# The gates of a gated DeltaNet layer: context and latents in the two halves of each 32-row group, 256 columns instead of 512

## The chip, the core and the metric

The program runs on one core of a Trainium2 chip. The metric is the device time of one launch in microseconds (us). The core's engines work side by side, each through its own list of instructions in a fixed order: TensorE (PE in the profile, its weight loads PEld), VectorE (DVE), ScalarE (ACT), GpSimd (POOL) and SyncE, whose queue (SP) issues nearly all DMAs. An instruction that waits for another engine holds up everything behind it on its own engine.

## The reference, cut to what matters

Two layers run on 256 context tokens and 256 latent tokens of width 1024. Layer 0 is a state-space layer with an MLP, layer 1 a bidirectional gated DeltaNet (the recurrence layer) with an MLP. The change lies in the gates of layer 1: for every token, two directions and 16 heads, a write strength `beta` and a decay `g`, and the running sum of `g` within chunks of 64 tokens.

```python
gl = rest[..., qk + vd:].astype(f32).reshape(b, l, 2, 2, GDN_VALUE_HEADS)
beta = jax.nn.sigmoid(gl[:, :, 0])
g = -jnp.exp(a_log) * jax.nn.softplus(gl[:, :, 1] + dt_bias)
...
g_b = jnp.cumsum(blocks(g), axis=-1)          # blocks of GDN_CHUNK = 64 tokens
decay = jnp.exp(jnp.where(incl, g_b[..., :, None] - g_b[..., None, :], -jnp.inf))
lower = jnp.where(strict, jnp.einsum('nbhcd,nbhsd->nbhcs', k_beta, k_b) * decay, 0.0)
t_mat = triangular_solve(lower + eye, eye)    # then u, w, k_end, and the scan over chunks
```

The gate values `gl` are 64 columns of one product `h @ w_in` (kind of gate x direction x head).

## The kernel before

Layer 1 is one call of `gdn_phase`. It makes tasks, Python generators that emit instructions: one projection per 128 columns of `w_in` (`gdn_proj`, 48 of them and one for the gates), the work on each projection's result (`post_qk`, `post_z`, `post_v`, each with a five-tap convolution in `conv_silu`), the gates (`gdn_gates`), the triangular inverse per pair of heads and direction (`gdn_t`, 16 of them), the chunk recurrence per head (`gdn_chain`), the read-out and the output projection.

`drive` chooses the order in which the tasks emit. It keeps a model of every engine's time (`Clock.issue`, lines 170 to 255: a cost for each instruction from its number of columns), and takes the task that the model says can start first, by priority among equals; a scheduler then fixes each engine's list from these priorities. The list is static. When the model's cost of some instructions changes, the order of all that is emitted later can change, on all engines.

The gates go as follows. `gdn_proj` (line 1609) makes 48 matmuls of 256 columns, first on the latents, then on the context, into the two halves of one bank `proj` [128, 512]: the 128 rows are 4 groups of 32 (beta of direction 0 and 1, decay of direction 0 and 1), the 512 columns are the tokens. Only 16 rows of each 32 are heads; the other 16 have zero weights. `gdn_gates` (line 1506) works on [128, 512] tiles named `gt`: sigmoid and softplus by an exponential and a polynomial of the logarithm (lines 1522 to 1549, on DVE but for the exponential), the running sum `GR` by two scans over 32 rows (line 1558) with a mask that POOL sets (lines 1555 and 1556), its copy to DRAM `grd` by four DMAs (line 1564), its transposes `gtp` on PE (line 1568), and the sums at each chunk's end, `glp`, by 16 small products (line 1575). From these come `gpn`, `gn`, `egs`, `neg`, `egl` and `vsc`, small tiles that scale the recurrence.

Who needs them: each `gdn_t` loads a tile `X` from `grd` by DMAs of SP, adds a mask on POOL, subtracts `gpn` on DVE, takes the exponential on ACT, and then makes five rounds of a DVE transpose `T`, a product `ap` on PE, a mask on DVE (`A`) and a product `up`. It also needs `kks`, made from `kk`, the products of the normalised keys. The keys are normalised in `post_qk`: convolution (`cacc`, four steps of DVE), `kc`, transposes `kp`, `kn` and its sums of squares `kss` on ACT, `krs` on POOL, `kn` scaled on ACT, transposes `kTp` on PE.

Three more helpers set the pace. `w_split` turns each loaded weight block `wraw` into `whi` (ACT) and `wlo` (in this layer four POOL instructions of 256 columns per block); a projection needs both. A projection's bank (`proj`, or `c2` for the first ten in turn with it) is free again when ACT has copied it to one of two convolution buffers (`pp`). The projections come in the order q0, q1, gates, z0, z1, k0, v0, v1, k1, v2, v3 and so on, k, v and q standing for keys, values and queries.

Of the kernel before, what the change touches and what calls it, by code (L numbers as in the profile page):

```python
# [8 lines left out]
F32 = mybir.dt.float32  # L9
# [4 lines left out]
OP = mybir.AluOpType  # L14
# [964 lines left out]
def host_weights(i):  # L979
    a = {n: np.asarray(v) for n, v in i.items()}  # L980
    out = {}
    w = a["s5_w_glu"][0].reshape(8, 128, 2, 4, 256)
    out["w_glu"] = w.transpose(3, 0, 1, 2, 4).reshape(4, 4, 2, 128, 512).transpose(0, 1, 3, 2, 4).reshape(4, 4, 128, 1024)
    out["w1"] = a["mlp_w1"].reshape(2, 4, 2, 128, 8, 512).transpose(0, 4, 1, 3, 2, 5).reshape(2, 8, 4, 128, 1024)
    out["w2"] = a["mlp_w2"].reshape(2, 8, 4, 128, 1024)
    wi = a["gdn_w_in"][0]
    out["w_in"] = wi[:, :6144].reshape(8, 128, 48, 128).transpose(2, 1, 0, 3).reshape(48, 128, 1024)
    wg = np.zeros((1024, 4, 32), np.float32)
    wg[:, :, :16] = wi[:, 6144:].reshape(1024, 4, 16)
    out["w_gate"] = wg.reshape(8, 128, 128).transpose(1, 0, 2).reshape(128, 1024)  # L990
    gb = np.zeros((2, 4, 32), np.float32)
    gb[0, 2:, :16] = a["gdn_dt_bias"][0]
    gb[1, 2:, :16] = a["gdn_a_log"][0]
    out["gcol"] = gb.reshape(2, 128).T
    out["conv"] = a["gdn_conv_w"][0].reshape(5, 32, 128).transpose(2, 1, 0)
    out["onorm"] = a["gdn_onorm_w"][0].reshape(128, 1)
    out["w_out"] = a["gdn_w_out"][0].reshape(16, 128, 1024)
    out["fnorm"] = np.broadcast_to(a["final_norm_w"][None], (128, 1024))
    return {n: np.ascontiguousarray(v, dtype=np.float32) for n, v in out.items()}
# [428 lines left out]
def host_consts2():  # L1428
    c = np.zeros((128, NCONST2), np.float32)
    p = np.arange(128) % 64  # L1430
    J, I = p[:, None], np.arange(64)[None, :]
    for d in range(2):
        c[:, M_INC + 64 * d:M_INC + 64 * d + 64] = np.where((I >= J, I <= J)[d], 0.0, NEG)

        a, b = (J, I) if d == 0 else (I, J)
        c[:, M_U + 64 * d:M_U + 64 * d + 64] = (I == J) | ((a % 2 == 0) & (b == a + 1))

        i, j = (J, I) if d == 0 else (I, J)
        for n, s in enumerate((2, 4, 8, 16, 32)):
# [6 lines left out]
    c[:, M_G] = np.where(r % 32 >= 16, 0.0, np.where(r < 64, -1.0, 1.0))  # L1446
    c[:, M_G + 1] = (r % 32 < 16) & (r >= 64)
    return c


def host_layout2(i):
    out = host_weights(i)
    out["consts2"] = np.ascontiguousarray(host_consts2(), dtype=np.float32)
    return out


class K3(K2):
# [48 lines left out]
    def gdn_gates(self, tmp, o):  # L1506
        nc, V, G = self.nc, self.nc.vector, self.nc.gpsimd
        P, c2 = self.g, self.c2
        gc = tmp.tile([128, 2], F32, name="gc")
        nc.sync.dma_start(gc, self.I["gcol"])  # L1510
        ps, slot = o.pop("ps"), o.pop("slot")
        room = iter(("ub0", "ub1", "ub0", "ub1", "ub0", "ub1", "N", "N"))

        def t():
            tag = next(room)
            return (self.gb.tile([128, 512], F32, name="gt", tag=tag) if tag == "N" else
                    self.gw.tile([128, 512], F32, name="gt", tag=tag, bufs=NRB))


        gs, gm = c2[:, M_G:M_G + 1], c2[:, M_G + 1:M_G + 2]  # L1520
        s, a, e = t(), t(), t()
        V.tensor_scalar(s, ps, gs, gc[:, 0:1], op0=OP.mult, op1=OP.add)
        slot.give()
        V.scalar_tensor_tensor(a, s, -1.0, s, op0=OP.mult, op1=OP.max)
        nc.scalar.activation(e, a, AF.Exp, scale=-1.0)
        yield

        z, z2 = t(), t()
        q, r = a, t()
        V.tensor_scalar(z, e, 2.0, None, op0=OP.add)  # L1530
        V.reciprocal(z, z)
# [18 lines left out]
        GR = z2  # L1550
        V.tensor_copy(GR[0:64], lg[0:64])
        m = z
        for d in range(2):
            r = slice(64 + 32 * d, 96 + 32 * d)
            G.memset(m[r], 1.0)
            G.memset(m[r, (0 if d == 0 else 63):512:64], 0.0)
            f = lambda x: x[r] if d == 0 else bass.AP(tensor=x.tensor, offset=x[r].offset + 511, ap=[list(x[r].ap[0]), [-1, 512]])
            V.tensor_tensor_scan(f(GR), f(m), f(lg), 0.0, op0=OP.mult, op1=OP.add)
        self.grd = self.dram.tile([2, 16, 512], F32, name="grd")
        for d in range(2):  # L1560
            for h2 in range(2):
                r = 64 + 32 * d + h2
                dst = bass.AP(tensor=self.grd.tensor, offset=self.grd.offset + 8192 * d + 64 * h2, ap=[[1024, 8], [128, 8], [1, 64]])
                nc.sync.dma_start(dst, GR[r:r + 16:2].rearrange("p (c i) -> p c i", i=64))
        yield
        tp = self.tr("gtp")
        for b in range(4):
            nc.tensor.transpose(tp[:, b * 128:b * 128 + 128], GR[:, b * 128:b * 128 + 128], self.ident)
        lp = self.tr("glp")
        for k in range(8):  # L1570
            for d in range(2):
                c = k if d == 0 else (3 - k if k < 4 else 11 - k)
                last = c * 64 + (63 if d == 0 else 0)
                o = k * 32 + d * 16
                nc.tensor.matmul(lp[:, o:o + 16], GR[64:128, last:last + 1].to_broadcast([64, 128]),
                                 self.ident[64:128, 64 + 32 * d:64 + 32 * d + 16], start=(k == 0 and d == 0), stop=(k == 7 and d == 1),
                                 skip_group_check=True)
        gt = t().rearrange("p (a b c d) -> p a b c d", a=4, b=2, c=2)
        V.tensor_copy(gt.rearrange("p a b c d -> p (a b c d)"), tp)
        gl = t()[:, 0:256].rearrange("p (a b c) -> p a b c", a=8, b=2)  # L1580
        V.tensor_copy(gl.rearrange("p a b c -> p (a b c)"), lp[:, 0:256])

        self.gp = P.tile([128, 4, 2, 16], F32, name="gpn")
        V.tensor_tensor(self.gp, gt[:, :, 1, :, 0:16], gt[:, :, 0, :, 0:16], op=OP.subtract)
        self.egl = P.tile([128, 8, 2, 16], F32, name="egl")
        nc.scalar.activation(self.egl, gl, AF.Exp)

        gn = tmp.tile([128, 4, 2, 16], F32, name="gn")
        V.tensor_copy(gn, gt[:, :, 1, :, 0:16])
        self.egs = P.tile([128, 4, 2, 16], F32, name="egs")  # L1590
        self.vsc = P.tile([128, 4, 2, 16], F32, name="vsc")
        pr = lambda x: x.rearrange("p (a b) h -> p a b h", a=2)
# [15 lines left out]

    def gdn_proj(self, streams, out):

        while not self.wq:
            yield HOLD
        wh, wl = self.wq.pop(0)
        n, self.nproj = self.nproj, self.nproj + 1
        out["slot"] = slot = self.pslots[n % len(self.pslots) if n < NEARLY else 0]
        yield from slot.take()
        ps = self.bank("proj", "pr", bufs=NPR) if slot is self.pslots[0] else self.cb[-self.pslots.index(slot)]
        for n, s in enumerate(streams):
            o = ps if s is None else ps[:, 256 * s:256 * s + 256] if len(streams) > 1 else ps[:, 0:256]
            for dt in range(8):  # L1620
                self.mm3(o, wh[:, dt], wl[:, dt], self.cols(self.hh, dt, s), self.cols(self.hl, dt, s), dt == 0, dt == 7)
# [424 lines left out]
    def gdn_phase(self, tmp, gb, hp, new):  # L2046
        full, lat = (None,), (1,)
        I, T = self.I, Task
        st, blocks, pj, tasks, o = [dict() for _ in range(8)], [], [], [], {}
# [47 lines left out]
        g, j = g  # L2097
# [47 lines left out]
        dst = [hp.tile([128, 4, 1024], F32R, name=n, tag=n) for n in ("hh", "hl")]  # L2145
# [119 lines left out]
```

## Time and profile before

| what | us |
|---|---|
| median of three runs | 1602.71 |
| lowest and highest of the three | 1600.59 and 1606.34 |
| the profiled execution, as timed | 1608.33 |
| its span in the trace | 1606.5 |
| PE busy in the span | 1461.4 (91%) |
| DVE busy | 1098.4 (68%) |
| ACT busy | 775.2 (48%) |
| POOL busy | 652.0 (41%) |

The profile is one execution. Its timed value, 1608.33 us, is 1.8 us above its span and 5.6 us above the median of the runs. All times of the trace are us from the start of the span. Layer 1 begins at about 738 us and its output projection ends at about 1375 us. A busy share over the whole span says little here, as the stages have different limits; the stretches of 20 us below are read instead.

### The profile page before, as it was taken

To read this page: it belongs to the slowest core of one execution; us is meant where nothing else is said; L and a number is where in the kernel's file an instruction comes from. 1 tells how busy PE (TensorE), PEld (TensorE's weight loads), DVE (VectorE), ACT (ScalarE), POOL (GpSimd) and SP (SyncE) were. 2 spreads that over 40 slices of the span, in tenths; PEclk is the share of its full clock that TensorE was granted. 3 is DMA by queue.
4 is the path that set the end of the run, shared out by engine and by line. 5 is a ranking of instruction groups with operands and counts; after the bars stand their busy time and mean duration, and the time that the engine had idled before them with its cause. 6 is when DMAs were issued, how large, how long until landed. Compare 5 with 4: busy or idle time off the path is not lost. (4 is left out here: it accounts for less than half of the span.)

```text
span 1606.5 us, 31329 instructions
## 1 busy us (share of the span) xinstructions
PE 1461.4 (91%) x12370; PEld 1115.2 (69%) x12370; DVE 1098.4 (68%) x2036; ACT 775.2 (48%) x1635; POOL 652.0 (41%) x590
## 2 busy tenths in 40 slices
PE   6895689989999999996978998989998999989998
PEld 2474457768777777786756775767776665789997
DVE  6999877754334333448998876686978775666766
ACT  3262675534222223315456655656665755564443
POOL 4962026623333332335777543443543400024432
PEclk8897789989999999998889999989998999999999
DMA  8758725454444454422222211111121112535552
GB/s 286 255 195 200 141 86 184 151 183 134 163 162 166 163 187 161 152 91 66 90 70 67 67 54 48 50 51 54 61 70 38 45 58 79 188 127 194 185 186 92
DMA packets 76771, 200.77 MB, mean 125 GB/s; under 512 B 8784, under 2 KB 29008, under 8 KB 76368
## 3 DMA queue, kind: packets, MB, share of 16 engines
q1 hardware_dynamic: 76112, 197.78, 38.3%
q8 instruction: 97, 1.59, 0.4%
q10 hardware_dynamic: 512, 0.98, 0.2%
q14 instruction: 50, 0.41, 0.1%
HBM read 192.71 MB, written 6.03 MB: 124 GB/s over the span
## 5 line engine op out<-in xcount | busy, mean ns | idle before, releaser
L273 ACT CAST whi<-wraw 128x1024 fp32r<-128x1024 f32 x221 | 225.6, 1045 | 255.7 <-PE w L273 139.0
L273 POOL TENSOR_TENSOR wlo<-wraw,whi 128x256 fp32r<-128x256 f32 (+1 forms) x221 | 206.8, 963 | 270.7 <-ACT whi L273 253.2
L273 DVE TENSOR_TENSOR wlo<-wraw,whi 128x1024 fp32r<-128x1024 f32 (+1 forms) x189 | 223.4, 1210 | 81.5 <-ACT whi L273 80.6
L273 PE MATMUL w<-hh,whi 128*128 128x256 f32 (+1 forms) x512 | 170.4, 335 | 0.0
L273 PE MATMUL w<-hl,whi 128*128 128x256 f32 (+1 forms) x512 | 169.3, 332 | 0.0
L273 PE MATMUL w<-hh,wlo 128*128 128x256 f32 (+1 forms) x512 | 168.9, 332 | 0.0
L273 POOL TENSOR_TENSOR sq<-rl 128x512 f32<-128x512 f32 (+1 forms) x64 | 62.7, 980 | 216.1 <-ACT rl L273 212.1
L273 PE MATMUL w<-whi,h1h 128*128 128x512 f32 x384 | 148.9, 395 | 0.0
L273 PE MATMUL w<-whi,h1l 128*128 128x512 f32 x384 | 148.5, 390 | 0.0
L273 PE MATMUL w<-wlo,h1h 128*128 128x512 f32 x384 | 148.4, 389 | 0.0
L273 PE MATMUL proj<-hh,whi 128*128 128x256 f32 (+1 forms) x360 | 132.4, 368 | 7.4 <-ACT pp L273 6.7
L273 DVE TENSOR_TENSOR ma<-w,g 128x512 f32<-128x512 f32 x96 | 65.3, 687 | 103.0 <-PE w L273 102.9
L273 PE MATMUL proj<-hh,wlo 128*128 128x256 f32 (+1 forms) x360 | 127.8, 355 | 1.2 <-POOL wlo L273 1.2
L273 PE MATMUL proj<-hl,whi 128*128 128x256 f32 (+1 forms) x360 | 127.3, 354 | 0.0
L273 POOL TENSOR_TENSOR xr<-xr,ma 128x512 f32<-128x512 f32 x56 | 82.2, 1471 | 95.1 <-DVE ma L273 95.1
L273 DVE SCALAR_TENSOR_TENSOR cacc<-pp,cw,cacc 128x520 f32<-128x520 f32 (+1 forms) x128 | 112.3, 879 | 9.6 <-ACT cacc L273 8.0
L273 ACT ACTIVATE v<-c,vsc 64x128 f32<-64x128 f32 x224 | 80.7, 362 | 62.8 <-PE c L273 57.7
L273 PEld LDWEIGHTS w<-hh,whi 128*128 128x128 f32 x512 | 98.0, 192 | 18.3 <-DVE wlo L273 4.2
L273 DVE TENSOR_TENSOR h1l<-sq,h1h 128x512 fp32r<-128x512 f32 (+1 forms) x64 | 36.3, 568 | 104.5 <-POOL sq L273 102.1
L273 PEld LDWEIGHTS w<-hl,whi 128*128 128x128 f32 x512 | 98.5, 192 | 10.5 <-issue 1.9
L273 PEld LDWEIGHTS w<-hh,wlo 128*128 128x128 f32 x512 | 98.3, 192 | 9.8 <-issue 0.8
L273 POOL TENSOR_TENSOR rstd<-ms,mhalf 128x1 f32<-128x1 f32 (+2 forms) x22 | 17.3, 788 | 179.1 <-DVE ms L273 163.4
(316 smaller groups left out, 3492.2 us busy)
## 6 DMA issues: line engine op xcount, KB each, us to landing
wraw<-in_w_dram SPq DMA_DIRECT2D x128, 512.0 KB, 4.5
adaw<-in_ada_w_dram SPq DMA_DIRECT2D x92, 512.0 KB, 4.8
wraw<-in_w_in_dram SPq DMA_DIRECT2D x48, 512.0 KB, 3.2
wraw<-in_w_glu_dram SPq DMA_DIRECT2D x32, 512.0 KB, 3.4
wraw<-in_w_out_dram SPq DMA_DIRECT2D x16, 512.0 KB, 3.4
Kt<-kd SPq DMA_DIRECT2D x32, 128.0 KB, 6.5
X<-grd SPq DMA_DIRECT2D x32, 128.0 KB, 3.2
V<-in_ada_w_dram SPq DMA_DIRECT2D x4, 512.0 KB, 5.2
```

What stands on the lines that cost most here:

```text
L273: r = f(*args, **kw)
```

## The change

The context tokens' gates keep 16 rows of each group of 32, and the latents' take the other 16, so that a gate tile is [128, 256] with no idle rows. The weights' columns move to the upper 16 of each group on the host; the context's 24 matmuls read the weights from 16 columns further on, so that their results land in the lower 16 rows and zeros in the upper ones (the last of its eight slices has only 112 columns), and the latents' 24 add theirs in the same bank. The context comes first now. Bias, decay and sign constants are filled for both halves. All work from line 1522 to the scans is on 256 columns; `grd` is written by eight DMAs of half the size; PE makes two transposes `gtp` instead of four; `gpn` and `gn` take two instructions each, one per half.

```diff
-            return (self.gb.tile([128, 512], F32, name="gt", tag=tag) if tag == "N" else
-                    self.gw.tile([128, 512], F32, name="gt", tag=tag, bufs=NRB))
+                    self.gw.tile([128, 512], F32, name="gt", tag=tag, bufs=NRB))[:, 0:256]
...
-        V.tensor_scalar(s, ps, gs, gc[:, 0:1], op0=OP.mult, op1=OP.add)
+        V.tensor_scalar(s, ps[:, 0:256], gs, gc[:, 0:1], op0=OP.mult, op1=OP.add)
...
-            G.memset(m[r, (0 if d == 0 else 63):512:64], 0.0)
+            G.memset(m[r, (0 if d == 0 else 63):256:64], 0.0)
...
-                r = 64 + 32 * d + h2
-                nc.sync.dma_start(dst, GR[r:r + 16:2].rearrange("p (c i) -> p c i", i=64))
+                for s in range(2):
+                    r = 64 + 32 * d + 16 * s + h2
+                    nc.sync.dma_start(dst, GR[r:r + 15:2].rearrange("p (c i) -> p c i", i=64))
...
-        for b in range(4):
+        for b in range(2):
             nc.tensor.transpose(tp[:, b * 128:b * 128 + 128], GR[:, b * 128:b * 128 + 128], self.ident)
...
-        V.tensor_tensor(self.gp, gt[:, :, 1, :, 0:16], gt[:, :, 0, :, 0:16], op=OP.subtract)
+        for s in range(2):
+            V.tensor_tensor(self.gp[:, 2 * s:2 * s + 2], gt[:, :, 1, :, s], gt[:, :, 0, :, s], op=OP.subtract)
...
-        V.tensor_copy(gn, gt[:, :, 1, :, 0:16])
+        for s in range(2):
+            V.tensor_copy(gn[:, 2 * s:2 * s + 2], gt[:, :, 1, :, s])
...
+                    wide = 128 if s or dt < 7 else 112
+                    lh, ll = [w.rearrange("p a b -> p (a b)")[:, 128 * dt + 16 - 16 * s:128 * dt + 16 - 16 * s + wide] for w in (wh, wl)]
+                    for m, (l, x) in enumerate(((lh, self.hh), (lh, self.hl), (ll, self.hh))):
+                        nc.tensor.matmul(o[0:wide], l, self.cols(x, dt, s), start=n == dt == m == 0, stop=n == 1 and dt == 7 and m == 2,
...
-            j = proj(I["w_gate"], (1, 0), 0, o)
+            j = proj(I["w_gate"], (0, 1), 0, o)
```

The model's costs of these instructions change with their width, and so the lists of all engines differ from the gates to the end of layer 1. Three places follow.

On DVE, behind the scans and the convolution of v0 (`cacc`), before: `kss` belongs to k0, `X` to the first pair of heads, `cacc_6965` and `vc_6964` to v1, `cacc_7076` to k1.

```order
L273 COPY gt_6992<-gtp_6970 128x512
L273 SCALAR_TENSOR_TENSOR cacc_6965<-pp0_6450,cw_6446,cacc_6965 128x520
L273 TENSOR_TENSOR gpn_6996<-gt_6992 128x128
L273 COPY gn_7000<-gt_6992 128x128
L273 TENSOR_SCALAR kss_7035<-kss_7035 128x4
L273 SCALAR_TENSOR_TENSOR cacc_6965<-pp0_6450,cw_6446,cacc_6965 128x520
L273 TENSOR_TENSOR X_7168<-X_7168,gpn_6996 128x512
L273 COPY egs_7002<-gn_7000 64x4x16 x4
L273 TENSOR_TENSOR X_7171<-X_7171,gpn_6996 128x512
L273 SCALAR_TENSOR_TENSOR vc_6964<-cth_6966,cacc_6965 128x2x64 x4
```

The same place after (`vc_6940` is v0's, `cacc_7023` and `vc_7022` are v1's, `cacc_7083` is k1's):

```order
L273 COPY egs_6918<-gn_6915 64x4x16 x4
L273 SCALAR_TENSOR_TENSOR vc_6940<-cth_6942,cacc_6941 128x2x64 x4
L273 SCALAR_TENSOR_TENSOR cacc_7023<-pp0_6450,cw_6446,cacc_7023 128x520 x3
L273 COPY gt_6908<-glp_6889 128x256
L273 SCALAR_TENSOR_TENSOR cacc_7023<-pp0_6450,cw_6446,cacc_7023 128x520
L273 TENSOR_TENSOR X_7131<-X_7131,gpn_6910 128x512
L273 TENSOR_TENSOR vsc_6919<-gt_6908,gpn_6910 64x4x16 x4
L273 TENSOR_TENSOR X_7134<-X_7134,gpn_6910 128x512
L273 SCALAR_TENSOR_TENSOR vc_7022<-cth_7024,cacc_7023 128x2x64 x4
L273 TENSOR_SCALAR kss_6998<-kss_6998 128x4
L273 SCALAR_TENSOR_TENSOR cacc_7083<-pp1_6452,cw_6446,cacc_7083 128x520 x4
```

`kss` moved behind the first pair's two `X`, `vsc` and v1's `vc`; the convolution of k1 follows it at once.

On ACT, the same stretch before (`whi_7028` is v3's weight block, `proj_6931` is k1's projection):

```order
L273 COPY kn_6962<-kp_6957 128x512
L273 ACTIVATE sq_7037,kss_7035<-kn_6962 128x128 x4
L273 CAST whi_7028<-wraw_6777 128x1024
L273 COPY pp1_6452<-proj_6931 128x256
L273 COPY pp1_6452<-proj_6931 128x4x64
L273 ACTIVATE cth_6966<-cacc_6965 128x520
L273 ACTIVATE kn_6962<-kn_6962,krs_7036 128x128 x4
L273 ACTIVATE cacc_7076<-pp1_6452,cw_6446 128x520
L273 ACTIVATE X_7168<-X_7168 128x512
```

And after (`whi_7057` is v3's block, `proj_7008` is k1's projection):

```order
L273 ACTIVATE sq_7000,kss_6998<-kn_6980 128x128
L273 ACTIVATE vsc_6919<-vsc_6919 128x128
L273 ACTIVATE X_7134<-X_7134 128x512
L273 ACTIVATE sq_7000,kss_6998<-kn_6980 128x128 x2
L273 ACTIVATE kn_6980<-kn_6980,krs_6999 128x128 x4
L273 COPY vs0_7038<-vt_7039 128x512
L273 CAST whi_7057<-wraw_6777 128x1024
L273 COPY pp1_6452<-proj_7008 128x256
L273 COPY pp1_6452<-proj_7008 128x4x64
L273 ACTIVATE cacc_7083<-pp1_6452,cw_6446 128x520
```

The split of v3's weights and the copy of k1's projection to its convolution buffer stood ahead of the scaled keys `kn`; now they stand behind them.

On PE, the transposes `kTp` of k0's keys before, in the projection of v3 (`proj_7148`), behind eight of its 24 matmuls:

```order
L273 MATMUL proj_7148<-hh_3052,wlo_7029 128x512
L273 MATMUL proj_7148<-hh_3052,whi_7028 128x512
L273 MATMUL proj_7148<-hl_3053,whi_7028 128x512
L273 MATMUL kTp_7081<-consts_63,kn_6962 128x2x64 x4
L273 MATMUL proj_7148<-hh_3052,wlo_7029 128x512
```

And after, in the projection of v2 (`c2_6468`), behind ten of its 24:

```order
L273 MATMUL c2_6468<-hh_3052,wlo_6989 128x512
L273 MATMUL c2_6468<-hh_3052,whi_6988 128x512
L273 MATMUL kTp_7072<-consts_63,kn_6980 128x2x64 x2
L273 MATMUL c2_6468<-hl_3053,whi_6988 128x512
L273 MATMUL kTp_7072<-consts_63,kn_6980 128x2x64
```

They come 22 projection matmuls earlier in PE's list (14 of v2 and 8 of v3).

## Rows read from the trace of the kernel before

**Rows 1.** Engines by stretch: stretch, length, each engine's busy us, clock, DMA, GB/s
```profile
core 0: us, PE busy (x) PEld busy (x) DVE busy (x) ACT busy (x) POOL busy (x), PEclk, DMA share, GB/s
760.00:780.00 20.00, 18.03 (x74) 14.60 (x75) 19.52 (x25) 9.29 (x23) 19.70 (x28) 0.91 0.24 80
...
940.00:960.00 20.00, 20.00 (x234) 13.83 (x231) 14.24 (x34) 12.36 (x31) 11.16 (x12) 1.00 0.09 28
```

**Rows 2.** Timeline of DVE: start, us, engine, line, operation, count, [idle before and releaser]
```profile
743.29 1.37 DVE L273 TENSOR_TENSOR hl<-hf,hh 128x512 fp32r<-128x512 f32 x1 [1.55 <-ACT hh L273]
...
758.22 3.35 DVE L273 RECIPROCAL gt<-gt 128x512 f32<-128x512 f32 x1
...
761.50 0.41 DVE L273 SCALAR_TENSOR_TENSOR zs<-zth,c 128x256 f32<-128x256 f32 x1
...
765.72 4.53 DVE L273 SCALAR_TENSOR_TENSOR gt<-gt 128x512 f32<-128x512 f32 x4
...
774.11 4.07 DVE L273 SCALAR_TENSOR_TENSOR cacc<-pp,cw,cacc 128x520 f32<-128x520 f32 x4
...
781.98 3.25 DVE L273 TENSOR_TENSOR_SCAN gt<-gt 32x512 f32<-32x512 f32 x2
...
790.82 3.05 DVE L273 SCALAR_TENSOR_TENSOR vc<-cth,cacc 128x128 f32<-128x128 f32 x4
793.79 0.68 DVE L273 COPY gt<-gtp 128x512 f32<-128x512 f32 x1
...
795.40 0.15 DVE L273 TENSOR_SCALAR kss<-kss 128x4 f32<-128x4 f32 x1
...
805.06 0.90 DVE L273 SCALAR_TENSOR_TENSOR kc<-cth,cacc 128x128 f32<-128x128 f32 x4
...
820.98 1.64 DVE L273 TENSOR_TENSOR U<-N,c 128x512 f16<-128x512 f32 x1
```

**Rows 3.** Groups of one tile: shortest, median, longest ns, first and last start
```profile
L273 DVE SCALAR_TENSOR_TENSOR gt<-gt x9: 692/1106/1784, 754.8 to 772.5; 128x512 f32<-128x512 f32 x9
...
L273 DVE TENSOR_TENSOR vsc<-gt,gpn x4: 210/214/222, 804.3 to 804.8; 64x64 f32<-64x64 f32 x4
...
L273 DVE COPY gt<-glp x1: 418/418/418, 803.3 to 803.3; 128x256 f32<-128x256 f32 x1
```

**Rows 4.** One more group, of tile X
```profile
L273 DVE TENSOR_TENSOR X<-X,gpn x16: 672/678/1734, 796.1 to 1216.9; 128x512 f32<-128x512 f32 x16
```

**Rows 5.** Timeline of POOL
```profile
772.24 3.79 POOL L273 TENSOR_TENSOR wlo<-wraw,whi 128x256 fp32r<-128x256 f32 x4
...
795.63 2.11 POOL L273 TENSOR_TENSOR krs<-kss,mhalf 128x4 f32<-128x4 f32 x1 [1.91 <-DVE kss L273]
```

**Rows 6.** Timeline of ACT
```profile
792.23 1.03 ACT L273 CAST whi<-wraw 128x1024 fp32r<-128x1024 f32 x1
793.16 0.64 ACT L273 COPY pp<-proj 128x256 f32<-128x256 f32 x2
...
797.77 1.28 ACT L273 ACTIVATE kn<-kn,krs 128x128 f32<-128x128 f32 x4 [0.89 <-POOL krs L273]
```

**Rows 7.** Timeline of PE
```profile
791.34 4.89 PE L273 MATMUL glp<-consts,gt 64*128 64x16 f32 x32
...
801.67 0.40 PE L273 MATMUL proj<-hh,whi 128*128 128x512 f32 x1
...
803.84 0.63 PE L273 MATMUL kTp<-consts,kn 128*128 128x128 f32 x4 [0.17 <-DVE gt L273]
...
813.10 0.50 PE L273 MATMUL proj<-hh,whi 128*128 128x512 f32 x1 [3.49 <-ACT pp L273]
...
824.98 0.58 PE L273 MATMUL ap<-T,nb 128*128 128x64 f16 x8 [3.62 <-DVE T L273]
```

**Rows 8.** Timeline of PE, later in the layer
```profile
990.39 0.70 PE L273 MATMUL c<-S,kt 128*64 128x128 f32 x4 [4.98 <-DVE S L273]
```

**Rows 9.** Timeline of SP, the DMA queue
```profile
783.64 2.99 SPq L273 DMA_DIRECT2D grd<-gt  x4
```

More of the change, by code (lines that the diff above doesn't have):

```diff
@@ L988, in host_weights @@
     wg = np.zeros((1024, 4, 32), np.float32)
-    wg[:, :, :16] = wi[:, 6144:].reshape(1024, 4, 16)
+    wg[:, :, 16:] = wi[:, 6144:].reshape(1024, 4, 16)
     out["w_gate"] = wg.reshape(8, 128, 128).transpose(1, 0, 2).reshape(128, 1024)
     gb = np.zeros((2, 4, 32), np.float32)
-    gb[0, 2:, :16] = a["gdn_dt_bias"][0]
-    gb[1, 2:, :16] = a["gdn_a_log"][0]
+    for r in (slice(0, 16), slice(16, 32)):
+        gb[0, 2:, r] = a["gdn_dt_bias"][0]
+        gb[1, 2:, r] = a["gdn_a_log"][0]
     out["gcol"] = gb.reshape(2, 128).T
@@ L1445, in host_consts2 @@
     r = np.arange(128)
-    c[:, M_G] = np.where(r % 32 >= 16, 0.0, np.where(r < 64, -1.0, 1.0))
-    c[:, M_G + 1] = (r % 32 < 16) & (r >= 64)
+    c[:, M_G] = np.where(r < 64, -1.0, 1.0)
+    c[:, M_G + 1] = r >= 64
     return c
@@ L1555, in gdn_gates @@
             G.memset(m[r], 1.0)
-            G.memset(m[r, (0 if d == 0 else 63):512:64], 0.0)
-            f = lambda x: x[r] if d == 0 else bass.AP(tensor=x.tensor, offset=x[r].offset + 511, ap=[list(x[r].ap[0]), [-1, 512]])
+            G.memset(m[r, (0 if d == 0 else 63):256:64], 0.0)
+            f = lambda x: x[r] if d == 0 else bass.AP(tensor=x.tensor, offset=x[r].offset + 255, ap=[list(x[r].ap[0]), [-1, 256]])
             V.tensor_tensor_scan(f(GR), f(m), f(lg), 0.0, op0=OP.mult, op1=OP.add)
@@ L1561, in gdn_gates @@
             for h2 in range(2):
-                r = 64 + 32 * d + h2
-                dst = bass.AP(tensor=self.grd.tensor, offset=self.grd.offset + 8192 * d + 64 * h2, ap=[[1024, 8], [128, 8], [1, 64]])
-                nc.sync.dma_start(dst, GR[r:r + 16:2].rearrange("p (c i) -> p c i", i=64))
+                for s in range(2):
+                    r = 64 + 32 * d + 16 * s + h2
+                    dst = bass.AP(tensor=self.grd.tensor, offset=self.grd.offset + 8192 * d + 64 * h2 + 512 * s, ap=[[1024, 8], [128, 4], [1, 64]])
+                    nc.sync.dma_start(dst, GR[r:r + 15:2].rearrange("p (c i) -> p c i", i=64))
         yield
         tp = self.tr("gtp")
-        for b in range(4):
+        for b in range(2):
             nc.tensor.transpose(tp[:, b * 128:b * 128 + 128], GR[:, b * 128:b * 128 + 128], self.ident)
@@ L1572, in gdn_gates @@
                 c = k if d == 0 else (3 - k if k < 4 else 11 - k)
-                last = c * 64 + (63 if d == 0 else 0)
+                last = c % 4 * 64 + (63 if d == 0 else 0)
                 o = k * 32 + d * 16
                 nc.tensor.matmul(lp[:, o:o + 16], GR[64:128, last:last + 1].to_broadcast([64, 128]),
-                                 self.ident[64:128, 64 + 32 * d:64 + 32 * d + 16], start=(k == 0 and d == 0), stop=(k == 7 and d == 1),
+                                 self.ident[64:128, 64 + 32 * d + 16 * (c // 4):64 + 32 * d + 16 * (c // 4) + 16], start=(k == 0 and d == 0), stop=(k == 7 and d == 1),
                                  skip_group_check=True)
-        gt = t().rearrange("p (a b c d) -> p a b c d", a=4, b=2, c=2)
-        V.tensor_copy(gt.rearrange("p a b c d -> p (a b c d)"), tp)
+        gt = t().rearrange("p (a b c s d) -> p a b c s d", a=2, b=2, c=2, s=2)
+        V.tensor_copy(gt.rearrange("p a b c s d -> p (a b c s d)"), tp[:, 0:256])
         gl = t()[:, 0:256].rearrange("p (a b c) -> p a b c", a=8, b=2)
@@ L1609, in gdn_proj @@
     def gdn_proj(self, streams, out):
+        nc = self.nc
         while not self.wq:
@@ L1618, in gdn_proj @@
         for n, s in enumerate(streams):
-            o = ps if s is None else ps[:, 256 * s:256 * s + 256] if len(streams) > 1 else ps[:, 0:256]
+            o = ps if s is None else ps[:, 0:256]
             for dt in range(8):
-                self.mm3(o, wh[:, dt], wl[:, dt], self.cols(self.hh, dt, s), self.cols(self.hl, dt, s), dt == 0, dt == 7)
+                if len(streams) == 1:
+                    self.mm3(o, wh[:, dt], wl[:, dt], self.cols(self.hh, dt, s), self.cols(self.hl, dt, s), dt == 0, dt == 7)
+                else:
+                    wide = 128 if s or dt < 7 else 112
+                    lh, ll = [w.rearrange("p a b -> p (a b)")[:, 128 * dt + 16 - 16 * s:128 * dt + 16 - 16 * s + wide] for w in (wh, wl)]
+                    for m, (l, x) in enumerate(((lh, self.hh), (lh, self.hl), (ll, self.hh))):
+                        nc.tensor.matmul(o[0:wide], l, self.cols(x, dt, s), start=n == dt == m == 0, stop=n == 1 and dt == 7 and m == 2,
+                                         skip_group_check=True)
                 if dt == 7 and n == len(streams) - 1:
```

## The prediction

> **What bounds the kernel now.** I read the busy times by stretch first, then the timelines of DVE, ACT, POOL and PE where the gates lie, then the waits. The gates of layer 1 stand in a stretch in which DVE works without a pause: 19.52 of 20 us, with POOL at 19.70 and PE at 18.03 [rows 1]. From about 750 to 905 us DVE is the limit. From 940 us on PE is (20.00 of 20 us, with DVE at 14.24 [rows 1]). So a microsecond that DVE saves among the gates can reach the end, if the work behind it moves up; a microsecond saved on ACT or POOL cannot. The reader should see in the timeline of DVE that the gates' operations are a row of 512-column operations between 754 and 786 us, that the same kinds of operation take far longer beside a POOL weight split than alone, and where `kss` stands [rows 2, 3, 5].
>
> **The change part by part.** *The width.* An operation of DVE with two inputs takes 0.69 us on 512 columns at its shortest [rows 3] and 0.41 on 256 [rows 2]: 0.28 less, and 0.13 that does not depend on the width. There are eleven (the nine of rows 3 and two products): 11 x 0.28 = 3.1. The reciprocal takes 3.35 [rows 2]; half of what lies above 0.13 is 1.6. The two scans take 3.25 [rows 2]: 1.5. The copy of `gtp` falls from 0.68 to 0.42, by the copy of `glp` that has 256 columns today [rows 2, 3]: 0.26, as much for the first operation on `proj`, and I take half of that for each of the four that read SBUF: 1.1 together. `gpn` and `gn` become two instructions each, at about 0.21 as for the small `vsc` [rows 3]: 0.2 more. The sum is 3.1 + 1.6 + 1.5 + 1.1 - 0.2 = 7.1 us of DVE.
>
> The bounds of this term come from the operations beside POOL. Four of the nine took 4.53 us, 1.13 each [rows 2], the median is 1.11 [rows 3]; only about three of the eleven ran alone. If the others keep their time, the two-input term is 0.8 instead of 3.1 and the sum 4.8. If they halve, it is about 6 and the sum 10. I take 7.1, for the rows show both: four operations of 128 columns take 0.90 us alone, 0.23 each, and 3.05 beside POOL, 0.76 each, while those of 520 columns take 1.02 beside POOL (4.07 for four) [rows 2]. Going from 520 columns to 128 saves 0.26 there, so the width still counts, but weakly.
>
> The Trainium skill (SBUF — State Buffer, "SBUF: two separate sides") says that a DVE operation with two SBUF inputs and a GpSimd operation that reads SBUF take an exclusive lock for the whole instruction. By that rule a contended operation costs what POOL's instruction costs, whatever its own width, and the sum would be 4.8, the lower bound above; the rows agree in that both get slower, and not in that the width is without effect.
>
> *What else gets smaller or larger.* ACT's exponential, POOL's mask and two of PE's four transposes halve; none of these engines is the limit, and the gain is none. PE's 48 gate matmuls stay 48 of 256 columns. That the context comes first costs nothing: its last normalised piece, 1.37 us long on DVE [rows 2], is ready before the gates' projection has the weights it waits for, since two query projections stand ahead; without that cover it would cost those 1.4 us. SP issues eight DMAs to `grd` instead of four: four took 2.99 us [rows 9], so 3 more. On SP one weight load stands between them and the four loads of `X`, and more behind. They have room, as the scans end 7 us earlier and `X` is now used on DVE behind v1's convolution; without it the 3 us would delay POOL's mask add.
>
> *What is moved, and takes it back.* Two places.
>
> First, the scans. Before, they end at 785.2 (781.98 + 3.25 [rows 2]). After, 6.9 us of the gates' saving lies ahead of their end, and three of k0's four `kc` (0.7 to 2.3 us by the two rows of such operations, I take 1.2) go behind them: 777.1. But the last columns of their mask are set by POOL behind a weight split that ends at 776.03 (772.24 + 3.79 [rows 5]), so the scans run from about 776.3 to 777.9. That costs 0.8.
>
> Second, `kss`. Before, it comes 10.2 us behind the scans' end (795.40 [rows 2]). After, this stands ahead of it in addition: three `kc` (0.7 to 2.3), one `cacc` (1.0), two `X` (2 x 0.68 [rows 4]), the four `egs` and four `vsc` (8 x 0.21 [rows 3]), the copy of `glp` (0.42 [rows 3]) and v1's four `vc` (0.9 to 3.05 [rows 2]): 6.1 to 9.8 us. So `kss` falls at 777.9 + 10.2 + 6.1 to 9.8 = 794 to 798. I take 797, since its last squares on ACT now stand behind both exponentials of `X`. It is not earlier than before, although 7 us were saved ahead of it.
>
> And now the next thing on DVE, the convolution of k1, hangs on it. The copy of k1's projection to `pp` stood ahead of `kn` on ACT (793.16, with `kn` at 797.77 [rows 6]); now it stands behind. From `kss` the chain is `krs` 2.11 [rows 5], `kn` 1.28 [rows 6], a copy `vs` of about 0.6 (by the `pp` copy, 0.64 [rows 6]), the weight cast 1.03, the `pp` copy 0.64 and the first convolution step on ACT, about 0.7 (likewise): 6.4 us, in which DVE has nothing else in its list. Its bounds are 5.4, if `krs` takes half, and 6.4. So DVE starts k1's convolution at 803.4 and its `kc` at about 808, where before `kc` starts at 805.06 [rows 2].
>
> PE meets the same chain. It reaches `kTp` ten matmuls into v2 at about 795 (`glp` began right behind that place at 791.34 and takes 4.89 [rows 7]; after, `glp` stands ahead, and some of PE's own waits are shorter), and stands there until `kn` is there, at 800.5: a new wait of 5 to 6 us. Before, `kTp` ran at 803.84 with no wait to speak of [rows 7]. After it come 20 matmuls up to `kk` instead of 16, at 0.27 (eight from 801.67 to 803.84 [rows 7]). So `kk` comes at about 807 against 808: nothing is gained there.
>
> The first inverse is then due. Before, its first `U` starts at 820.98 [rows 2], 15.9 us behind `kc`. After, v2's four `vc` and two `cacc` (2.9 to 5.0 us) stand behind it instead of ahead: 808 + 15.9 - 4 = 820, or up to 3 earlier where waits go. These 3 to 5 us are still owed to DVE, which remains the limit. But both `U` now stand side by side, so that the wait of PE for the first `T`, 3.62 us [rows 7], and the one behind it should shrink. I give that 2 us.
>
> The sum: 7.1 saved, less 0.8 at the mask, less 6.4 at k1, plus 2 at the inverse: about 2 us less (4.8 to 10 saved gives between 0.4 slower and 5.8 faster with the 5.4 for the chain). Against the profiled execution: 1608.33 - 2 = 1606.3. That execution is 5.6 above the median of the runs, so on their scale 1602.71 - 2 = **1600.7 us**, within 0.3% (4.8 us), which is about what a measurement of this kernel can tell from no change.
>
> **The rivals.** *Faster: the inverse carries, not DVE's total.* If both inverses of the first pair begin 3 to 5 us earlier and the owed convolutions fit into DVE's slack later (6 of 20 us free from 940 on [rows 1]), the time follows the inverse: 5, and with the 2 above 7 us less, about 1596. For it: PE is the limit later. Against: DVE stays full for 80 us behind, so owed work delays the next projections. 0.24.
>
> *Slower: PE's new wait at `kTp`.* PE stands 5 to 6 us in the middle of v2, where before it had projections to run. If its later waits, 3.49 for the `pp` copy and 3.62 for `T` [rows 7], stay, this is added in full: 6 us more, about 1608. It decides by when v3's projection begins: before at 801.67 [rows 7]; if after it begins later than about 807, the loss is there. For it: `krs` and `kn` cannot come before `kss`, and 0.76 instead of 0.23 for each `vc` puts `kss` at 798. 0.18.
>
> *The lists later on.* All engines' lists differ up to 1300 us. Before, at one place PE waits 4.98 us behind a tile `X` that came late [rows 8]. Such a wait can go or come: 5 us either way, 1596 or 1606 to 1608. 0.07 each.
>
> **How the numbers follow.** The forecast, about 2 us less with bounds of 1597 to 1605: 0.44. Faster by more than 0.3%: 0.24 + 0.07 = 0.31. Slower: 0.18 + 0.07 = 0.25. The range takes in both neighbours and the two bounds of the width term, 1591 (10 saved, the inverse carrying) to 1610 (4.8 saved, PE's wait added).
>
> **What would show it.** In the profile after: two-input gate operations of 0.41 alone and 0.7 to 0.9 beside POOL, some 7 us less for all of them; a wait of DVE of 5 to 7 us ahead of k1's first `cacc`, ended by ACT; a wait of PE of 5 us or more at `kTp`; `kss` at 796 to 798. I am wrong if `kss` comes well before 794, if DVE's wait there is under 3 us, or if the stretch from 900 us on differs by more than the first 100 us do.

## The result, and the profile after

The changed kernel takes 1631.41 us (median of 4 runs, 1626.68 to 1634.10), beside 1604.22 for the kernel before (now of 4 runs, 1600.59 to 1606.34): a ratio of 1.0167, with an interval of 1.0144 to 1.019. It is 27 us slower. The forecast was 1600.7, with a range that ended at 1610.

I read the first 100 us first, since the forecast was made of them. Windows of the kernel after, as [rows 1] has them for before:

```profile
core 0: us, PE busy (x) PEld busy (x) DVE busy (x) ACT busy (x) POOL busy (x), PEclk, DMA share, GB/s
760.00:780.00 20.00, 19.80 (x105) 16.33 (x103) 17.58 (x27) 7.61 (x15) 19.63 (x29) 1.00 0.23 83
940.00:960.00 20.00, 20.00 (x227) 14.12 (x227) 13.24 (x31) 13.27 (x36) 10.06 (x12) 1.00 0.16 54
```

In the first of them DVE is busy 17.58 us instead of 19.52, and PE 19.80 instead of 18.03; in the second PE is full as before. The layer begins 5 us earlier in this execution, so the windows do not hold quite the same work. Timeline of DVE after, the rows that answer [rows 2]:

```profile
738.18 1.38 DVE L273 TENSOR_TENSOR hl<-hf,hh 128x512 fp32r<-128x512 f32 x1 [1.55 <-ACT hh L273]
...
753.89 1.75 DVE L273 RECIPROCAL gt<-gt 128x256 f32<-128x256 f32 x1
...
757.68 2.58 DVE L273 SCALAR_TENSOR_TENSOR gt<-gt 128x256 f32<-128x256 f32 x3
...
764.61 2.23 DVE L273 COPY gt<-gt 64x256 f32<-64x256 f32 x1
...
772.79 1.77 DVE L273 TENSOR_TENSOR_SCAN gt<-gt 32x256 f32<-32x256 f32 x2 [1.49 <-POOL gt L273]
...
792.61 0.17 DVE L273 TENSOR_SCALAR kss<-kss 128x4 f32<-128x4 f32 x1 [0.62 <-ACT sq L273]
797.96 3.90 DVE L273 SCALAR_TENSOR_TENSOR cacc<-pp,cw,cacc 128x520 f32<-128x520 f32 x4 [5.18 <-ACT cacc L273]
802.56 0.90 DVE L273 SCALAR_TENSOR_TENSOR kc<-cth,cacc 128x128 f32<-128x128 f32 x4 [0.70 <-ACT cth L273]
...
813.04 0.68 DVE L273 TENSOR_TENSOR U<-N,c 128x512 f16<-128x512 f32 x1
```

The last piece of the layer's input, `hl`, comes at 738.18 in this execution and at 743.29 in the one of before [rows 2], though the stages ahead are the same; over all the profiles of this study it lies between 736 and 747. So the layer is best compared from that piece on. Counted so, `kss` comes after 54.4 us (forecast 53.7, from 797), `kc` of k1 after 64.4 (forecast 64.7), the first `U` after 74.9 (forecast 73.7 to 76.7; before 77.7). DVE's new wait ahead of k1's convolution is 5.18 us. Up to here the times on DVE are almost exactly those foretold. PE is where it went otherwise. Its timeline after:

```profile
794.38 0.62 PE L273 MATMUL kTp<-consts,kn 128*128 128x128 f32 x2 [2.13 <-ACT kn L273]
...
811.07 0.51 PE L273 MATMUL proj<-hh,whi 128*128 128x512 f32 x1 [1.49 <-ACT pp L273]
...
828.06 0.63 PE L273 MATMUL up<-U,A 64*64 64x64 f16 x16 [10.22 <-DVE A L273]
```

The wait at `kTp` is 2.13 us instead of 5 to 6, and in place of the waits of [rows 7] for `T` there is one of 10.22 for `A`, ahead of the next projection in the list. DVE makes that `A` only at 827.33, behind four `vc`, four `cacc` and an `X`, though PE had done its part (`ap`) by 817.4. Still, all this comes to 7 us at the recurrence: the first state update `S` comes 173.2 us after the layer's input (911.4 - 738.2), where before it comes after 166.0. The layer's end, however, comes after 889.3 us (1627.5 - 738.2), where before it comes after 863.2. Most of the 26 us are lost later.

### The profile page after: what moved, and what is told of

It reads as the page before. It is cut to its first block, busy times and chain, and to the rows that moved or that the text cites. A ratio compares the mean times of both kernels' runs of the same rounds, so it can differ in the third digit from the quotient of the medians.

```text
span 1627.5 us, 31370 instructions
## 1 busy us (share of the span) xinstructions
PE 1465.3 (90%) x12368; PEld 1112.0 (68%) x12368; DVE 1099.6 (68%) x2038; ACT 776.1 (48%) x1635; POOL 651.4 (40%) x590
## 4 chain that ended last, share of the span: by engine, by line
PE 64%; DVE 18%; ACT 5%; issue 4%; DMA 4%; POOL 4%; SPq 1%; POOLq 0%; DVEq 0%; ACTq 0%
PE w L273 32%; PE proj L273 9%; PE c L273 7%; PE ada L273 3%; PE wo L273 3%; DVE cacc L273 2%; POOL wlo L273 2%; DVE U L273 1%; DVE W L273 1%; PE glu L273 1%; PE up L273 1%; DVE wlo L273 1%; PE qs L273 1%; DMA adaw<-in_ada_w_dram 1%; DVE kc L273 1%
## 5 line engine op out<-in xcount | busy, mean ns | idle before, releaser
L273 DVE SCALAR_TENSOR_TENSOR cacc<-pp,cw,cacc 128x520 f32<-128x520 f32 (+1 forms) x128 | 116.6, 912 | 9.9 <-ACT cacc L273 8.3
L273 ACT ACTIVATE rl<-w 128x512 f32<-128x512 f32 (+1 forms) x64 | 31.3, 489 | 120.4 <-PE w L273 110.8
```

Source lines behind the costliest of these rows:

```text
L273: r = f(*args, **kw)
```

## The experiments

**Width and lists apart.** The change does two things at once. It narrows the gates' instructions, and as their costs in the planner change, every engine's list is made anew to the end of the layer. Two kernels take these apart. Each instruction is recorded as it is written, and at the end every engine is tied to a given order, by edges that order the issue and wait for nothing (the planner's steps are given too):

```diff
+def hold_lists(tc):
+    raw, at = zlib.decompress(base64.b85decode(LISTS)), 0
+    for _ in range(5):
...
+        for a, b in zip(rows, rows[1:]):
+            tc.add_manual_dep(EMIT[b], EMIT[a].name, mybir.DependencyInfo(mybir.DependencyClass.NoSync, mybir.DependencyReason.DATA),
+                              reason="list")
...
         tile_backbone(tc, *args)
+        hold_lists(tc)
```

`narrow_old_lists`: narrow gates, order of the kernel before.

> The narrow gates of the kernel after, with the order of every engine held to that of the kernel before (the gates' instructions stand where their wide forms stood, the two and four added ones right behind their fellows). Theory A (the loss of some 27 us comes from the lists that were made anew, from about 1056 us on, and not from the gates' own work): 1594 to 1606 us, that is the kernel before less the 2 to 7 us that DVE saves at the gates. Theory B (the loss comes from waits that the narrow gates bring themselves in the first 100 us, such as the PE wait of 10.2 us for A at 817, and is carried on): 1620 to 1635 us.

Measured: 1598.79 us, ratio to the kernel before 0.9962 (0.9945 to 0.9978). Once more, beside other kernels:

> The same kernel as narrow_old_lists, beside the other sets of lists on one chip: the narrow gates with the order of the kernel before. Theory A: 0.3 to 0.6% under the kernel before once more, 1594 to 1602 us; should the first result have been chance, 1601 to 1608 us.

Measured: 1602.82 us, 0.9978 (0.9961 to 0.9996). That is just outside the 1594 to 1602 expected and inside the range named for chance, though the interval still ends below 1. The narrow gates by themselves make the kernel 0.2 to 0.4% faster, 7 and 3 us by the medians of the two measurements (1605.65 and 1606.09 before). This is the version that beats both kernels.

`wide_new_lists`: wide gates, order of the kernel after.

> The wide gates of the kernel before, with the order of every engine held to that of the kernel after. Theory A (lists): 1628 to 1642 us, the kernel after plus the 2 to 7 us of the wider gates. Theory B (the narrow gates' own waits): 1598 to 1610 us, like the kernel before.

Measured: 1630.55 us, 1.0163 (1.0141 to 1.0186), which cannot be told from the kernel after. So the lists alone cost some 25 us, and under these lists the width is worth nothing that these runs can tell: the wide gates bring the first `S` 7.2 us later after the layer's input (180.4 against 173.2), and the end 0.5 us later (889.8 against 889.3). Theory B, the narrow gates' own waits, falls.

**How much a new set of lists can cost.** One number of the planner, the moment at which it lets TensorE start the layer, is shifted. No instruction changes.

```diff
-GDN0 = 803.4465179647354
+GDN0 = 803.4465179647354 + (-1.7)
```

> The kernel before with one number of the planner changed: the moment at which the planner lets TensorE start the layer is set 1.7 us earlier. The computation is the same, only the lists are made anew. Theory A (a new set of lists can cost or give 20 us and more by itself): the time differs from the kernel before by more than 5 us, and rather upwards, 1606 to 1640 us. Theory B: within 4 us of the kernel before, 1600 to 1608 us.

Measured: 1626.59 us, 1.0138 (1.0115 to 1.0161). The wide kernel loses 21 us by this alone. The other way (theories A1 and A2 in this and one later expectation are explained in the next part):

> The kernel before (wide gates) with the planner's start moment 1.7 us later: 108 state updates ahead of the last key convolution. Theory A1: 1606 to 1620 us, clearly under before_plan_m17 (1627, 122 updates). Rival A2: around 1628 us.

Measured: 1624.48 us, 1.0125 (1.01 to 1.015), outside the range of A1. The kernel after, with the same shifts:

> The kernel after with the same number of the planner set 1.7 us earlier: the same computation with lists made anew. Theory A: the time moves by more than 5 us, 1600 to 1640 us, most likely downwards since 1631 would be a poor draw. Theory B (the narrow gates cost it whatever the lists): 1626 to 1636 us.

Measured: 1631.43 us, 1.0173 (1.0145 to 1.02): no better draw, against my guess, and in the range that stood for theory B. This run by itself does not tell the theories apart; the two kernels with held lists do.

> The kernel after (narrow gates) with the planner's start moment 1.7 us later: 112 state updates ahead of the last key convolution. Theory A1: 1606 to 1622 us, within 8 us of before_plan_p17, since lists count for more than the width of the gates. Rival A2: around 1630 us.

Measured: 1614.17 us, 1.006 (1.0042 to 1.0078): in the range of A1, but 10 us from `before_plan_p17` instead of within 8. The lists of the kernel before lie at the good end of what this planner makes. Those of the kernel after are in the slower half, but no outlier: of the seven other sets of this study that the planner made freely, five are faster, one is equal and one is slower.

**Is it one place in the lists?** I compared `after` with `narrow_old_lists`, whose instructions are the same. In the kernel after, the convolution of the value head 12 is done at 1159 on DVE, and its product `vc` follows only at 1184.87, behind rows of the recurrence that wait for PE (its other input, `cth`, was ready on ACT by 1160.1); the last pair's `kc` comes at 1235.20. Rows of DVE, kernel after:

```profile
1157.85 1.56 DVE L273 SCALAR_TENSOR_TENSOR cacc<-pp,cw,cacc 128x520 f32<-128x520 f32 x1
...
1180.18 0.35 DVE L273 SCALAR_TENSOR_TENSOR oa<-qs,egs,oa 128x128 f32<-128x128 f32 x1 [1.46 <-PE qs L273]
1181.04 0.60 DVE L273 SCALAR_TENSOR_TENSOR S<-S,egl,c 128x128 f32<-128x128 f32 x2 [0.51 <-PE c L273]
1182.97 0.29 DVE L273 TENSOR_TENSOR oa<-oa,op 128x128 f32<-128x128 f32 x1 [1.32 <-PE op L273]
...
1184.87 0.89 DVE L273 SCALAR_TENSOR_TENSOR vc<-cth,cacc 128x128 f32<-128x128 f32 x4
...
1235.20 3.29 DVE L273 SCALAR_TENSOR_TENSOR kc<-cth,cacc 128x128 f32<-128x128 f32 x4
```

The same two products with the old lists:

```profile
1135.91 1.51 DVE L356 SCALAR_TENSOR_TENSOR vc<-cth,cacc 128x128 f32<-128x128 f32 x2
...
1192.94 3.06 DVE L356 SCALAR_TENSOR_TENSOR kc<-cth,cacc 128x128 f32<-128x128 f32 x4
```

They come 49 and 42 us earlier. Of the layer's 192 state updates, 102 stand ahead of that last `kc` in the old lists and 118 in the kernel after. So I made theory A1, that this place sets the time, against A2, that lists scatter whatever stands there, and picked three draws by it.

> The kernel after with the planner's start moment 3.0 us later, a set of lists picked by one place in it: on DVE 100 of the layer's 192 state updates (rows S) stand ahead of the last pair's key convolution kc, against 102 in the kernel before and 118 in the kernel after. Theory A1 (the loss is that the last pairs' convolutions stand too far behind the recurrence on DVE): 1596 to 1608 us. Rival A2 (lists scatter, and this place has nothing to do with it): around 1628 us like the four other new lists, 1620 to 1636.

Measured: 1619.28 us, 1.0079 (1.0049 to 1.011), with 100 updates ahead: between the two theories.

> The kernel after with the planner's start moment 5.5 us earlier: 132 state updates stand ahead of the last key convolution on DVE, the most of the lists looked through. Theory A1: slower than the kernel after, 1633 to 1655 us. Rival A2: around 1628 us, 1620 to 1636.

Measured: 1639.63 us, 1.0221 (1.0198 to 1.0245), with 132 ahead: as A1 says.

> The kernel after with the planner's start moment 0.5 us later: 106 state updates stand ahead of the last key convolution on DVE, and 80 ahead of the value convolution of the pair before (86 in the kernel before, 98 in the kernel after). Theory A1: 1598 to 1614 us. Rival A2: around 1628 us, 1620 to 1636.

Measured: 1607.95 us, 1.0028 (1.0007 to 1.0048), with 106 ahead: as A1 says.

Then the place itself was moved, by a rule that holds two chains back in the plan until those convolutions are placed:

```diff
+        for n, t in ((8, vv[12]), (9, kq[7])):
+            fl[n].after += [t]
```

> The kernel after_plan_m17 with one rule more for the planner: the first chain of the pair numbered 4 waits in the plan for the value projection's convolution of head 12, and its second chain for the last key convolution. The lists are those of after_plan_m17 up to the late stretch; then 110 instead of 126 state updates stand ahead of the last key convolution on DVE. Theory A1 (late convolutions cost the time): 1608 to 1622 us, and kc of the last pair 15 us or more earlier. Rival A2: 1626 to 1636 us like after_plan_m17, or worse, since the chains are held back.

Measured: 1629.99 us, 1.0174 (1.0117 to 1.023).

> The kernel after with the same rule and its own start moment: 112 instead of 118 state updates ahead of the last key convolution, 112 instead of 122 ahead of the value convolution that follows and 116 instead of 130 ahead of the last one; the lists up to there as in the kernel after. Theory A1: 1612 to 1626 us. Rival A2: 1626 to 1636 us.

Measured: 1629.59 us, 1.0167 (1.0126 to 1.0208). In both the last `kc` did come earlier, by 33 and 17 us after the layer's input, and in both the time stayed. A1 falls as the sole cause: in `after_plan_p30` and `rule_m17` this `kc` comes within 4 us of where it does in the kernel before, and their ends come 12 and 20 us later than its end. What the rule costs by holding the chains back was not measured, so the place may still count for a part. All the profiles side by side, worked out from their timelines, each from the layer's input on. The medians were taken beside the kernel before, which had 1603.3 to 1606.1:

| kernel | updates ahead of the last `kc` | last `kc`, us | last output matmul `wo`, us | end, us | median, us |
|---|---|---|---|---|---|
| narrow_old_lists | 102 | 454.2 | 657.7 | 857.6 | 1598.79 |
| narrow_old_lists_again | 102 | 454.0 | 659.7 | 860.0 | 1602.82 |
| old_steps_all | 106 | 463.1 | 661.2 | 862.5 | 1603.12 |
| before | 102 | 457.4 | 663.1 | 863.2 | 1604.22 |
| after_plan_p05 | 106 | 462.1 | 664.2 | 865.5 | 1607.95 |
| after_plan_p17 | 112 | 482.1 | 674.1 | 874.0 | 1614.17 |
| old_steps_half | 112 | 476.3 | 674.0 | 874.4 | 1619.63 |
| after_plan_p30 | 100 | 458.1 | 674.8 | 874.7 | 1619.28 |
| before_plan_p17 | 108 | 473.5 | 679.7 | 879.7 | 1624.48 |
| old_steps_quarter | 112 | 469.3 | 683.3 | 882.8 | 1624.68 |
| rule_m17 | 110 | 461.4 | 683.1 | 883.4 | 1629.99 |
| rule_00 | 112 | 479.6 | 684.3 | 884.2 | 1629.59 |
| after_plan_m17 | 126 | 494.5 | 687.3 | 887.4 | 1631.43 |
| after | 118 | 497.0 | 689.7 | 889.3 | 1631.41 |
| before_plan_m17 | 122 | 496.6 | 689.4 | 889.4 | 1626.59 |
| wide_new_lists | 118 | 499.8 | 690.1 | 889.8 | 1630.55 |
| after_plan_m55 | 132 | 505.9 | 697.8 | 897.7 | 1639.63 |

The stretch from the last `wo` to the end is 199 to 202 us in all of them, so the whole difference is made inside the recurrence layer.

**Which part of the list-making.** The planner takes the steps of all tasks one by one; a scheduler orders each engine's instructions behind it. The planner's steps of the kernel before (1718 in the layer) were recorded and taken again in the kernel after, in whole, to the half, and to the quarter, with the scheduler left free:

```diff
-        t = best[1]
+        t = todo[order.pop(0)] if order else best[1]
...
-        tasks = drive(self.clock, tasks, until=tt[7] + pj)
+        tasks = drive(self.clock, tasks, until=tt[7] + pj, steps=STEPS[0])
```

> The kernel after with all 1718 steps of the planner in the recurrence layer taken in the order of the kernel before, while the scheduler that orders each engine's instructions is left free (on DVE 1376 of 2038 instructions stand in one common order with the kernel before, 1214 for the kernel after). Theory P (the planner's steps carry the loss): 1597 to 1608 us. Theory Q (any set of lists that differs in so many places costs about 20 us, whoever made it): 1615 to 1630 us.

Measured: 1603.12 us, 0.9979 (0.9954 to 1.0004). All of the loss is gone, though 662 of DVE's 2038 instructions do not stand in one common order with the kernel before. That many rows differ is not what costs: theory Q falls.

> The kernel after with the first 860 of the planner's steps as in the kernel before, and the rest chosen by the planner itself. Theory P with late steps to blame: 1615 to 1632 us, like the kernel after; theory P with early steps to blame: 1597 to 1612 us. Theory Q: 1615 to 1630 us.

Measured: 1619.63 us, 1.008 (1.0051 to 1.011).

> The kernel after with the first 430 of the planner's steps as in the kernel before, and the rest chosen by the planner itself. Theory P, whichever steps are to blame: 1610 to 1632 us, no faster than with half of the steps. Theory Q: 1615 to 1630 us.

Measured: 1624.68 us, 1.0106 (1.0076 to 1.0137). The loss grows with the share of steps that are chosen anew: 16 us for the second half, 5 for the second quarter (not to be told from none, the intervals overlap), and 7 by the medians or 10 by the ratios for the first. Theory P holds, with early and late steps to blame both.

**Where the lists lose it.** From 1100 to 1300 us, kernel after, and then `narrow_old_lists`:

```profile
1100.00:1200.00 100.00, 88.63 (x993) 61.81 (x992) 71.70 (x158) 56.66 (x153) 40.73 (x42) 0.93 0.14 47
1200.00:1300.00 100.00, 91.29 (x1130) 63.55 (x1128) 74.21 (x167) 61.35 (x172) 38.03 (x41) 0.93 0.14 47
```

```profile
1100.00:1200.00 100.00, 94.88 (x1136) 70.02 (x1134) 83.25 (x183) 70.26 (x191) 50.54 (x54) 1.00 0.20 63
1200.00:1300.00 100.00, 93.86 (x1370) 67.01 (x1370) 79.63 (x194) 65.73 (x184) 32.38 (x33) 0.97 0.10 34
```

PE is busy 8.8 us less (179.92 against 188.74), does 2123 matmuls instead of 2506, and its granted clock is 0.93 instead of 0.985 in the mean: part of the stretch ran at 1.2 instead of 2.4 GHz. No engine is full. One pause of PE, with no projection in its list at that place, and the 10 us in and behind it:

```profile
1157.98 0.69 PE L273 MATMUL qs<-S,qt 128*64 128x128 f32 x4 [4.53 <-DVE oa L273]
```

```profile
1156.00:1166.00 10.00, 6.36 (x50) 4.53 (x51) 9.78 (x16) 3.43 (x8) 9.53 (x8) 0.50 0.01 2
```

PE had stood since 1153.45, and the granted clock fell to its lower level while it stood. Over the whole layer, from its input to the last `wo`, the kernel after, the kernel before and `narrow_old_lists`:

```profile
738.18:1427.90 689.72, 620.27 (x6444) 453.86 (x6442) 522.31 (x1066) 395.72 (x1002) 292.48 (x313) 0.94 0.20 66
743.29:1406.40 663.11, 607.80 (x6451) 451.64 (x6449) 518.62 (x1064) 395.01 (x1002) 293.04 (x313) 0.95 0.21 69
738.77:1396.50 657.73, 603.78 (x6448) 448.73 (x6447) 510.46 (x1066) 394.57 (x1002) 288.90 (x313) 0.96 0.21 69
```

So of the 26.6 us that the layer is longer than before, 14.1 are time in which PE is idle, and 12.5 are longer busy time for nearly the same matmuls. The clock records of the traces hold part of the latter: PE is busy at the lower level for 63.4 us, and for 50.5 before (43.6 in `narrow_old_lists`). At that level a projection matmul of 512 columns starts every 0.43 us instead of every 0.23, so about half of such time is lost: by estimate 6 us against the kernel before and 10 against `narrow_old_lists`.

To count all of it I took each matmul's time from its start to the next one's start, from 745 us on, less the median for its kind in the kernel before. These differences, those below the median included, sum to 134.4 us in the kernel before, 127.5 in narrow_old_lists and 158.1 in the kernel after. Of the 23.7 us between before and after, 12.2 lie in excesses of over 1 us, 3.0 in those of 0.3 to 1, and 8.5 in what is below 0.3: more than a third shows in no wait that a list of waits would name. Against narrow_old_lists, whose instructions are the same, the three parts are 14.6, 2.8 and 13.2, and of the last 7.2 lie in matmuls that began at the lower clock. The second comparison is the safer one, since a matmul missing from a trace lengthens one of these times: the trace of the kernel before has 25 records more than that of the kernel after, where the change explains 2, and narrow_old_lists has 3 fewer. The small losses are thus in good part the clock, and not small waits.

## Why the prediction was wrong, point by point

- *The width on DVE: right.* The sum was 7.1 us, with bounds of 4.8 and 10. The gates' operations on DVE (`gt`, `gpn`, `gn`) sum to 23.70 us in the trace of before and 16.62 after: 7.1 less. That it came out to the decimal is luck, for the shares were off. The eleven two-input operations gave 4.6 instead of 3.1 (11.45 to 6.87). The copies and the other one-input operations without the reciprocal, forecast at 1.1 (their parts add up to 1.04), cost 0.3, since one copy took 1.8 more (last section). With the order held, the width alone gives 7.6 in the old lists (23.70 to 16.13) and 6.2 in the new ones (22.77 to 16.62).
- *The scans behind POOL's mask: right* in that DVE waits there, 1.49 us ahead of the scans, ended by POOL. The forecast was 0.8.
- *`kss`, `kc` and the first `U`: right,* to within 1 us. *DVE's wait ahead of k1's convolution* was there, ended by ACT, at 5.18 us a little under its bounds of 5.4 to 6.4.
- *SP: right.* Its eight DMAs to `grd` took 2.7 us more than the four of [rows 9], where 3 were foretold, and POOL's two mask adds waited 0.52 and 0.88 us for `X` (4.33 before).
- *PE at `kTp` and at the inverse: wrong.* PE's wait at `kTp` was 2.13 instead of 5 to 6: counted from the layer's input, PE came there 2.4 us later than foretold and `kn` 1.0 earlier. The credit of 2 us for the two `U` side by side was not paid: the wait for the first `T` became one of 10.22 for `A`. This cost up to 7 us at the first `S`. That it decides nothing shows in `after_plan_m17`, which has its first `S` after 163.4 us, 2.6 earlier than the kernel before, and its end 24 later.
- *"The lists later on": the step that failed.* I saw that all lists differ up to 1300 us and sized this by a single row, the wait of 4.98 us in [rows 8]: 5 us either way, 0.07 each. Measured, with nothing but lists changed, it is 25 us (`wide_new_lists`) and 21 each (`before_plan_p17`, `before_plan_m17`). The sum of the first 100 us was treated as the forecast and the lists as a rival of it, where the lists were the larger term by far, and one with a sign. No set that the planner made anew, for wide gates or narrow, came out faster than the kernel before (1608 to 1640 us in eight sets made without a rule or old steps, that of the kernel after among them). A change that makes all lists anew should have been costed as a fresh draw from such sets against the one that the kernel happens to have. The trace of before could not show the width of that draw. But PE at 20.00 of 20 us with DVE at 14.24 [rows 1] hinted that little was left to win there and much to lose.
- *The rivals.* "The inverse carries" (about 1596) is not far from what the narrow gates bring with the old lists (1598.79 and 1602.82), but so is the forecast, and neither was made for those lists. "PE's new wait at `kTp`" would have given the right sign for a wrong reason, and a fifth of the size.
- *What would show it* named the outcome: the stretch from 900 us on differs by more than the first 100 us do (the end by 26 us, the first `U` by 3).

What stays open is why the planner's old steps are good. One feature, early convolutions of the last pairs, goes with short times over most of the table, but `rule_m17` has it and is slow, `after_plan_p30` has it and is 13 us over the kernel before, and `before_plan_p17` has it in part and is slow too.

## What to carry to other kernels

When an edit changes the costs that a planner or scheduler sees, it is two changes: hold the order of all engines (or take the planner's old steps again) to measure the edit, and shift a number of the planner that computes nothing to measure what a new order can do. Do both before blaming the edit, and keep the old order where it is the better one. In a kernel whose bound engine is nearly full, the order that it happens to have is part of its tuning, and a gain of a few microseconds did not survive its loss here.

## What was unexpected of the hardware

A copy that reads and writes SBUF can stand behind a train of POOL's operations. The gates' copy took 2.23 us after (row at 764.61 above), and 0.28 with the old lists, with POOL between two weight splits. Beside the slow one POOL ran this:

```profile
761.71 3.47 POOL L273 TENSOR_TENSOR wlo<-wraw,whi 128x256 fp32r<-128x256 f32 x4
765.12 1.57 POOL L273 MEMSET v<- 128x256 f32 x6
```

The copy ended at 766.84, just behind the last of six memsets (766.69). In `narrow_old_lists` another one-input operation met memsets in the same way: it took 2.82 us, where in the kernel after, with POOL idle, it took 0.29.

```profile
753.01 2.82 DVE L356 TENSOR_SCALAR gt<-gt 128x256 f32<-128x256 f32 x1 [0.81 <-ACT gt L356]
```

```profile
752.96 1.84 POOL L356 MEMSET nb<- 128x1024 f16 x2
754.74 0.95 POOL L356 MEMSET lo<- 128x1024 f16 x1
```

The Trainium skill (SBUF — State Buffer, "Who interferes with whom") states that a copy or a one-input operation in a two-port mode shares a port pair with GpSimd, and that the one that comes second is blocked until the other is finished. The rows agree, though the trace does not say in which mode these two ran, and show besides that several of POOL's instructions in a row can pass before DVE gets its turn.

Two-input operations behave otherwise. Groups of `gt` in the kernel after, with narrow_old_lists below (shortest, median, longest ns):

```profile
L273 DVE SCALAR_TENSOR_TENSOR gt<-gt x9: 417/820/845, 751.0 to 763.0; 128x256 f32<-128x256 f32 x9
```

```profile
L356 DVE SCALAR_TENSOR_TENSOR gt<-gt x9: 417/425/848, 750.0 to 766.4; 128x256 f32<-128x256 f32 x9
```

Alone they take 0.42, beside a weight split 0.82 to 0.85; the 512-column ones took 0.69 and 1.11 [rows 3]. So contention added about 0.42 us to either width. The prediction weighed the reading that a contended operation costs what POOL's costs, whatever its own width, which would have left the two-input term at 0.8 us. It was 4.6: the width counts beside POOL as it does alone. POOL's splits show why both can look true. Beside the 512-column operations (before) and the 256-column ones (after) they ran so:

```profile
765.37 4.33 POOL L273 TENSOR_TENSOR wlo<-wraw,whi 128x256 fp32r<-128x256 f32 x4
```

```profile
757.47 3.39 POOL L273 TENSOR_TENSOR wlo<-wraw,whi 128x256 fp32r<-128x256 f32 x4
```

That is 1.08 us for each of POOL's operations where DVE's took 1.13 (765.72 in [rows 2]), and 0.85 where they took 0.86 (row at 757.68 above). Each cost about what the other's cost, and both got shorter with DVE's width.
